# Input projections of an encoder layer as 2x2 block products with seven multiplications, in a phase of their own

## The chip, the cores and the metric

The kernel runs on one core of one Trainium2 chip. The metric is the device time of one execution in microseconds (us), the median of several runs. One further execution was profiled; rows and stage times come from it.

## The reference

One layer of a bidirectional encoder is applied with the same weights to two sequences, a prompt of 512 and a sample of 2048 tokens, all in float32, 1024 channels wide:

```python
h = rmsnorm(x, norm_pre)
z = h @ w_in                                  # 1024 -> 6656
pool_u, pool_g, q, k, v, attn_g, merge = split(z)   # 1024, 1024, 1024, 256, 256, 1024, 2048
pb = group_linear(windowed_mean(pool_u) - pool_u) * pool_scale * silu(pool_g)   # windows 2, 4, 8, 16
ab = windowed_attention(rope(q), rope(k), v, sink) * silu(attn_g)   # 16 heads, 4 kv heads, 64 wide, |i-j| <= 128
m = sigmoid(merge[:1024]) * (pb @ w_pool_proj) + sigmoid(merge[1024:]) * (ab @ w_attn_proj)
y = x + rmsnorm(m @ w_out, norm_post)
```

## The kernel before

Every float32 operand of a product is split into two parts, `hi` (rounded to the fp32r type of TensorE) and `lo` (the rest). `mm3` makes three products of each: hi x hi, hi x lo and lo x hi, lines 115 to 117. The split is `hi_lo`: a copy on ScalarE (L75) and a subtraction on VectorE (L76).

The tokens are worked in five blocks of 512, the prompt and four of the sample. A block is finished, from normalisation to output, before the next one begins. The normalised input `h` of a block lies in SBUF as 8 pairs of `hh`/`hl` tiles, 128 channels each. `unit` makes 128 output channels for the whole block: 8 pieces of 128 input channels, three products each, 24 products with a 128x128 weight tile as stationary operand and 512 tokens as moving one, summed in one PSUM bank, and then a `post` function. Weights are loaded from DRAM for each block again, 256 KB at a time (L82), and split again.

At the start `fold` multiplies the per-group maps of the pooling branch into the weights of `pool_u` and writes the product `wpool` to DRAM, 32 steps of six products of 256 columns.

A block runs in this order. `kv_phase` makes keys and values with tokens on the partitions, and transposes the keys. `q_units` makes and rotates the queries. Then attention runs: `grid` lays the steps of 16 groups (4 key heads x 4 query blocks of 128) into slots, and `mix` spreads other units evenly between them (queries of the next key head, `ag`, `ga`, `gp`, some `u`), 256 steps in all. A group computes scores (L334, L335), the masked maximum (L338), the exponentials (L340), scales them by the reciprocal sum (L353, L359 and L357), transposes them (L368), splits them into `pt`, and multiplies them by the values (L379, L380; results are added up in L387 to L390). The raw gates `ga` and `gp` go to DRAM and come back (L314, L433). After attention the block runs `ap_unit` (attention projection), the rest of `u_unit` with `pg_unit` (pooling branch), `pp_unit` (pooling projection) and `out_phase` (output projection, second norm, residual), 16 + 8 units and 64 steps. The statistics and the split of the next block's `h` are made meanwhile.

TensorE runs in the order in which the program is written; the last loop of `encoder` asks for the weights of the next `AHEAD = 2` items. The other engines' orders are set by a scheduler at compile time, from the same program. All transfers are issued by SyncE (SP), in one order.

## Time and profile before

| | us |
|---|---|
| median of 3 runs (2499.0 to 2502.37) | 2499.87 |
| span of the profiled execution | 2497.5 |
| TensorE busy | 2475.3 (99%) |
| VectorE busy | 1689.9 (68%) |
| ScalarE busy | 1381.8 (55%) |
| DMA, mean over the span | 129 GB/s, 322.60 MB |

The profiled execution's span lies 2.4 us below the median of the runs. Products overlap in the pipeline, so their durations add up to more than the busy time; distances between starts tell what one of them takes from the stream. L numbers are lines of the kernel before.

### The profile page before, as it was taken

What the parts mean: (1) busy time and instruction counts of PE and PEld (TensorE: products, weight loads), DVE (VectorE), ACT (ScalarE), POOL (GpSimd) and SP (SyncE); (2) the same over time, 40 slices, a digit from 0 to 9 for tenths busy, and PEclk for the clock granted to TensorE, in tenths of its full rate; (3) what the DMA queues carried; (4) which work ended last, traced back from release to release, by engine and by line L of the source; (5) the groups of instructions that cost most, each with busy time, mean ns of one, the idle gap of its engine ahead of it and who ended that gap; (6) DMA issues with size and microseconds to landing.
All of it is one profiled execution on the core that took longest, in us unless ns stands there. A gap on an engine that the chain in (4) does not pass through costs nothing.

```text
span 2497.5 us, 33882 instructions
## 1 busy us (share of the span) xinstructions
PE 2475.3 (99%) x11591; PEld 2039.2 (82%) x11591; DVE 1689.9 (68%) x3315; ACT 1381.8 (55%) x2831; POOL 117.7 (5%) x298
## 2 busy tenths in 40 slices
PE   8999999999999999999999999999999999999999
PEld 6888888878888888888888888888888878888887
DVE  5777756568777465777774657777746568776464
ACT  4777633437776333477763434776634357765342
POOL 0000100000000000000000000000000000000000
PEclk9999999999999999999999999999999999999999
DMA  7332473553224535522245445222454442334443
GB/s 231 98 93 91 140 232 108 169 167 94 85 95 130 173 101 162 179 89 89 85 127 177 127 150 164 89 85 89 133 167 141 142 153 81 91 89 155 131 160 106
DMA packets 179245, 322.60 MB, mean 129 GB/s; under 512 B 22144, under 2 KB 33664, under 8 KB 179072
## 3 DMA queue, kind: packets, MB, share of 16 engines
q1 hardware_dynamic: 179072, 320.43, 40.9%
q8 instruction: 91, 1.49, 0.2%
q14 instruction: 82, 0.67, 0.1%
HBM read 274.22 MB, written 46.14 MB: 128 GB/s over the span
## 4 chain that ended last, share of the span: by engine, by line
PE 95%; DMA 2%; DVE 1%; ACT 1%; issue 0%; SPq 0%; POOL 0%; DVEq 0%; POOLq 0%; ACTq 0%
PE ps_g L116 24%; PE ps_g L117 24%; PE ps_g L115 24%; PE ps_t L368 4%; PE ps_s L117 2%; PE ps_s L116 2%; PE ps_o L380 2%; PE ps_s L335 2%; PE ps_s L115 2%; PE ps_s L334 2%; PE ps_o L379 2%; PE ps_t L115 1%; PE ps_t L116 1%; PE ps_t L117 1%; DMA x<-in_x_sample 1%
## 5 line engine op out<-in xcount | busy, mean ns | idle before, releaser
L75 ACT CAST wh<-wr 128x512 fp32r<-128x512 f32 x776 | 478.6, 619 | 670.7 <-PE ps_g L116 326.7
L115 PE MATMUL ps_g<-hh,wh 128*128 128x512 f32 (+1 forms) x1920 | 770.0, 401 | 0.0
L117 PE MATMUL ps_g<-hh,wl 128*128 128x512 f32 (+1 forms) x1920 | 750.8, 391 | 0.3 <-DVE wl L76 0.3
L116 PE MATMUL ps_g<-hl,wh 128*128 128x512 f32 (+1 forms) x1920 | 749.8, 390 | 0.0
L76 DVE TENSOR_TENSOR wl<-wr,wh 128x512 fp32r<-128x512 f32 x776 | 531.0, 688 | 319.9 <-ACT wh L75 316.9
L117 PEld LDWEIGHTS ps_g<-hh,wl 128*128 128x128 f32 x1920 | 360.8, 188 | 82.3 <-DVE wl L76 1.0
L116 PEld LDWEIGHTS ps_g<-hl,wh 128*128 128x128 f32 x1920 | 361.7, 188 | 59.0
L115 PEld LDWEIGHTS ps_g<-hh,wh 128*128 128x128 f32 x1920 | 361.2, 188 | 57.7
L116 PE MATMUL ps_g<-A,wh 128*128 128x512 f32 x640 | 254.3, 397 | 0.0
L115 PE MATMUL ps_g<-A,wh 128*128 128x512 f32 x640 | 252.7, 395 | 0.0
L117 PE MATMUL ps_g<-A,wl 128*128 128x512 f32 x640 | 251.6, 393 | 0.0
L340 ACT ACTIVATE P<-ps_s,nm 128x384 f32<-128x384 f32 (+1 forms) x320 | 179.1, 560 | 123.8 <-DVE nm L338 121.6
L338 DVE CUSTOM_DVE_ANT_0 ps_s<-ps_s,mask,nsink 128x384 f32<-128x384 f32 (+1 forms) x320 | 190.0, 595 | 84.3 <-PE ps_s L335 81.9
L76 DVE TENSOR_TENSOR pt<-ps_t,pt 128x512 fp32r<-128x512 f32 x224 | 153.7, 687 | 32.5 <-ACT pt L75 29.3
L115 PEld LDWEIGHTS ps_g<-A,wh 128*128 128x128 f32 x640 | 120.2, 188 | 30.1
L117 PEld LDWEIGHTS ps_g<-A,wl 128*128 128x128 f32 x640 | 120.2, 188 | 29.0
L116 PEld LDWEIGHTS ps_g<-A,wh 128*128 128x128 f32 x640 | 120.2, 188 | 27.9
L368 PEld LDWEIGHTS ps_t<-ident,P 128*128 128x128 f32 x896 | 111.7, 141 | 29.5
L368 PE MATMUL ps_t<-ident,P 128*128 128x128 f32 x896 | 134.1, 272 | 0.0
L75 ACT CAST pt<-ps_t 128x512 fp32r<-128x512 f32 x168 | 97.1, 579 | 29.0 <-PE ps_t L368 28.9
L335 PE MATMUL ps_s<-ktl,q 128*128 128x384 f32 (+1 forms) x320 | 104.1, 325 | 0.0
L334 PE MATMUL ps_s<-kth,q 128*128 128x384 f32 (+1 forms) x320 | 103.7, 324 | 0.0
(240 smaller groups left out, 3278.1 us busy)
## 6 DMA issues: line engine op xcount, KB each, us to landing
wr<-in_w_q SPq DMA_DIRECT2D x80, 256.0 KB, 2.9
wr<-in_w_ag SPq DMA_DIRECT2D x80, 256.0 KB, 2.9
wr<-in_w_ga SPq DMA_DIRECT2D x80, 256.0 KB, 2.8
wr<-in_w_gp SPq DMA_DIRECT2D x80, 256.0 KB, 2.8
wr<-wpool SPq DMA_DIRECT2D x80, 256.0 KB, 2.7
wr<-in_w_ap SPq DMA_DIRECT2D x80, 256.0 KB, 3.2
wr<-in_w_pg SPq DMA_DIRECT2D x80, 256.0 KB, 2.7
wr<-in_w_pp SPq DMA_DIRECT2D x80, 256.0 KB, 2.9
```

What stands on the lines that cost most here:

```text
L75: (e.copy if e is A else e.tensor_copy)(hi, src)
L76: pick(key, 1).tensor_sub(lo, src, hi.bitcast(F32))
L115: T.matmul(o, lhsT=xs[0], rhs=ys[0], start=start, stop=False)
L116: T.matmul(o, lhsT=xs[0], rhs=ys[1], start=False, stop=False)
L117: T.matmul(o, lhsT=xs[1], rhs=ys[0], start=False, stop=stop)
L334: T.matmul(s, lhsT=q, rhs=kth[:, kv, kc], start=True, stop=False)
L335: T.matmul(s, lhsT=q, rhs=ktl[:, kv, kc], start=False, stop=True)
L338: V.tensor_tensor_reduce(s, s, mask[:, kb0 * 128:kb1 * 128], -1.0, nsink[:, H:H + 1], ALU.add, ALU.min, nm[:, h:h + 1])
L340: A.activation(P[:, 0:nk], s, AF.Exp, bias=nm[:, h:h + 1], scale=-1.0, accum_out=l[:, h:h + 1])
L368: T.transpose(tp[:, h * 128:(h + 1) * 128], pr[h][:, i * 128:(i + 1) * 128], cst["ident"])
L379: T.matmul(o, lhsT=v, rhs=pts[i][:, 0, :], start=i == 0, stop=False)
L380: T.matmul(o, lhsT=v, rhs=pts[i][:, 1, :], start=False, stop=i == kb1 - kb0 - 1)
```

## The change

The input projections are taken out of the block loop into a first phase. Weights are taken in 26 pairs of 128-wide units; a pair and a token block make a 2x2 by 2x2 block product: A is the pair's weights (two units by two halves of the 1024 input channels), B the block's `h` (two halves of the channels by two halves of the tokens). It is computed in Winograd's form of Strassen's scheme: seven products (M1 to M7) instead of eight, with sums S1 to S4 of weight blocks and T1 to T4 of input blocks as operands, and five additions behind them that use the PSUM bank's own accumulation where two products add up. Each product has 4 pieces of 128 channels and three matmuls each.

There are three token blocks over both sequences together: 768, 896 and 896 tokens, so the moving operand has 384, 448 and 448 columns. The seven moving operands of a block (`form`), split into hi and lo, lie in a fixed SBUF area, the `arena`. `h` is computed once per block, written to DRAM (`prep_h`) and read back in pieces. In the first block the weight sums are computed, split, and their split form is written to DRAM (`swd`); in the two later blocks it is loaded. The first two and the last two pairs run together as duos; in the last duo the operands of the next block are formed one by one.

Behind a pair a `Post` function finishes the result for all the block's tokens, and stores it in DRAM: `Rope` for keys and queries (rotation, split, 16 stores of 32 partitions), `Values` (transposes, split), `Silu`, `Gate` (sigmoid), `Pool` (window means times the gate). All 32 fold steps come ahead of the first pair.

The second phase takes the five blocks of 512 tokens again. Per key head `fetch_kv` loads split queries, keys, values and the attention gate. Attention is mixed with the pooling projection of the next block and the attention projection of the last one, 128 steps in all; the fifth block has 64. Then the output projection of the last block follows. The pooling result, the attention result and the half-finished merge go through DRAM, and are split as they come back (`put_set`).

```diff
+NPAIR = 26
+BLOCKS = ((0, 768), (768, 1664), (1664, 2560))
+HALF = 448
+ORDER = ("M1", "M6", "M2", "M5", "M7", "M3", "M4")
+WOP = {"M1": "A11", "M2": "A12", "M3": "S4", "M4": "A22", "M5": "S1", "M6": "S2", "M7": "S3"}
+XOP = {"M1": "B11", "M2": "B21", "M3": "B22", "M4": "T4", "M5": "T1", "M6": "T2", "M7": "T3"}
+SOPS = ("S2", "S1", "S3", "S4")
+XS = ("B11", "T2", "B21", "T1", "T3", "B22", "T4")
+NX = 7 * 2 * 4 * HALF
+AHEAD_H, AHEAD = 4, 3
+NW, NZ, NH, NR, NS_, NPB, NPT = 8, 6, 8, 2, 6, 8, 3
...
+    PS = {"g": 2, "s": 3, "t": 2, "o": 1}
...
+    arena = const.tile([128, NX], F32R, tag="arena", name="arena")
...
+    def prep_h(s, k):
+        a_, b = BLOCKS[s]
+        xk = ztile()
+        nc.sync.dma_start(xk[:, 0:b - a_], a["xt"][k, :, a_:b])
+        V.scalar_tensor_tensor(xk[:, 0:b - a_], xk[:, 0:b - a_], cst["gpre"][:, k:k + 1], rbc[s][:, 0:b - a_], ALU.mult, ALU.mult)
+        nc.sync.dma_start(hd[s][k], xk[:, 0:b - a_])
...
+        def piece(k, half):
+            t = htile()[:, 0:w]
+            nc.sync.dma_start(t, hd[s][k][:, half * w:(half + 1) * w])
+            return t
+
+        def put(r, k, src):
+            hi_lo(X[r][0][:, k, 0:w], X[r][1][:, k, 0:w], src)
+
+        for k in range(4):
+            if r == "B11":
+                put(r, k, piece(k, 0))
+            elif r == "B21":
+                put(r, k, piece(k + 4, 0))
+            elif r == "B22":
+                put(r, k, piece(k + 4, 1))
+            elif r == "T2":
+                b11, b12, b22 = piece(k, 0), piece(k, 1), piece(k + 4, 1)
+                V.tensor_sub(b12, b12, b11)
+                if k % 2 == 0:
+                    t2s["z"] = ztile()
+                t2 = t2s[k] = t2s["z"][:, k % 2 * 512:k % 2 * 512 + w]
+                V.tensor_sub(t2, b22, b12)
+                put("T2", k, t2)
...
+        def raw(self):
+            if self.R is not None:
+                return
+            self.R = self.p1.tile([128, 2048], F32, tag="R", bufs=NR, name="R")
+            for c0, c1, src in self.srcs:
+                if self.s > 0:
+                    c1 = min(c1, 1536)
+                nc.sync.dma_start(self.R[:, c0:c1], src[:, 0:c1 - c0])
+
+        def sums(self, n):
+            if n not in self.S:
+                a11, a12, a22, a21 = (self.R[:, i * 512:(i + 1) * 512] for i in range(4))
+                if n == "S1":
+                    op, x, y = V.tensor_add, a21, a22
+                elif n == "S3":
+                    op, x, y = V.tensor_sub, a21, a11
+                elif n == "S2":
+                    op, x, y = V.tensor_add, self.sums("S3"), a22
+                else:
+                    op, x, y = V.tensor_sub, a12, self.sums("S2")
+                t = self.p1.tile([128, 512], F32, tag="S", bufs=NS_, name="S")
+                op(t, x, y)
+                self.S[n] = t
+            return self.S[n]
+
+        def op(self, n):
+            self.raw()
+            if n[0] == "S" and self.s > 0:
+                w = wtile()
+                move(w, swd[self.n][SOPS.index(n)])
+                return w
+            src = self.sums(n) if n[0] == "S" else self.R[:, ("A11", "A12", "A22").index(n) * 512:][:, 0:512]
+            w = wtile()
+            hi_lo(w[:, 0, :], w[:, 1, :], src)
+            if n[0] == "S":
+                move(swd[self.n][SOPS.index(n)], w)
+            return w
...
+        for r in ORDER:
+            def f(r=r):
+                bank = {"M1": "A", "M2": "A", "M6": "B", "M5": "B", "M3": "B", "M7": "C", "M4": "C"}[r]
+                first = r in ("M1", "M6", "M7")
+                if first:
+                    st[bank] = psum(tags[bank])[:, 0:w]
+                acc = st[bank]
+                wt = pair.items[r].w
+                xh, xl = X[XOP[r]]
+                for k in range(4):
+                    c = slice(k * 128, (k + 1) * 128)
+                    mm3(acc, (wt[:, 0, c], wt[:, 1, c]), (xh[:, k, 0:w], xl[:, k, 0:w]), first and k == 0, k == 3, not first)
+                if r == "M1":
+                    st["s"] = htile()[:, 0:w]
+                    A.copy(st["s"], acc)
+                elif r == "M6":
+                    st["U2"] = htile()[:, 0:w]
+                    V.tensor_add(st["U2"], acc, st["s"])
+                elif r == "M2":
+                    post.start()
+                    for dst, c in post.dst(0, 0):
+                        post.first(dst, acc[:, c])
+                    post.done(0, 0)
+                elif r == "M5":
+                    st["U4"] = htile()[:, 0:w]
+                    V.tensor_add(st["U4"], acc, st["s"])
+                elif r == "M7":
+                    add(1, 1, acc, st["U4"])
+                elif r == "M3":
+                    add(0, 1, acc, st["s"])
+                else:
+                    add(1, 0, acc, st["U2"])
+                    post.finish()
+                if after is not None:
+                    after(r)
+            steps.append((pair.items[r], f))
...
+        def finish(self):
+            W = self.W
+            x1, x2 = (z[:, 0:W] for z in self.z)
+            cs, sn = rope[0][:, 0, 0:W], rope[0][:, 1, 0:W]
+            t1, t2 = ztile()[:, 0:W], ztile()[:, 0:W]
+            V.tensor_mul(t1, x1, cs)
+            V.tensor_mul(t2, x2, sn)
+            V.tensor_sub(t1, t1, t2)
+            V.tensor_mul(x2, x2, cs)
+            V.tensor_mul(x1, x1, sn)
+            V.tensor_add(x2, x2, x1)
+            for c, y in enumerate((t1, x2)):
+                hi = ztile(F32R)[:, 0:W]
+                lo = y.bitcast(F32R)
+                hi_lo(hi, lo, y)
+                for e, z in enumerate((hi, lo)):
+                    rows = slice((2 * e + c) * 32, (2 * e + c + 1) * 32)
+                    for h in range(4):
+                        move(self.to[rows, h, self.a:self.b], z[32 * h:32 * h + 32, :])
...
+        def finish(self):
+            for z, f in zip(self.z, self.fs):
+                nc.sync.dma_start(self.to[f][:, self.a:self.b], z[:, 0:self.W])
...
+                specs += [g[x] for x in (("q", "ag", "u0", "gp", "u1", "ga") if kv < 3 else ("q", "u0", "ag", "u1", "gp", "ga"))]
+            pairs = [Pair(p1, s, n, sr) for n, sr, _ in specs]
+            duos = [[0, 1]] + [[i] for i in range(2, NPAIR - 2)] + [[NPAIR - 2, NPAIR - 1]]
+            extra = {3: vals.tr_steps()}
+            if nxt:
+                extra[12] = [(None, lambda s=s: stats(s + 1))]
+                extra[15] = [(None, lambda s=s: prep_r(s + 1))]
+                for k in range(NKT):
+                    extra[16 + k // 2] = extra.get(16 + k // 2, []) + [(None, lambda s=s, k=k: prep_h(s + 1, k))]
+            prog.append((None, lambda s=s: load_rope(p1, s, "rope_k")))
+            for duo in duos:
+                if duo[0] == 2:
+                    prog.append((None, lambda s=s: load_rope(p1, s, "rope_q")))
+
+                def after(r, last=nxt and duo[-1] == NPAIR - 1, s=s):
+                    if last:
+                        form(s + 1, XOP[r])
+                steps = [pair_steps(pairs[i], specs[i][2], j, after if j + 1 == len(duo) else None) for j, i in enumerate(duo)]
+                ahead = [i for i in range(duo[-1] + 1, min(duo[-1] + 2, NPAIR))]
+                for j in range(7):
+                    for x in steps:
+                        prog.append(x[j])
+                    if j == 0:
+                        prog.append((None, lambda ahead=ahead, pairs=pairs: [pairs[i].raw() for i in ahead if len(ahead) == 1]))
+                for i in duo:
+                    prog += extra.get(i, [])
...
+    SETS = [(region(o, 8, 512), region(o + 4096, 8, 512)) for o in (0, 8192)]
+    QT = [region(16384 + i * 2048, 4, 512) for i in range(2)]
+    KT = [[region(20480 + i * 1536 + e * 768, 768) for e in range(2)] for i in range(2)]
+    VT = [region(23552 + i * 768, 6, 128) for i in range(2)]
...
+        def put_set(n, k, src):
+            t = htile()
+            nc.sync.dma_start(t, src)
+            hi_lo(SETS[n][0][:, k, :], SETS[n][1][:, k, :], t)
...
+            move(q, qd[kv][:, :, g0:g0 + TB])
+            for r in range(2):
+                rows = slice(64 * r, 64 * r + 64)
+                move(kh[rows, 0:c], kd[0:64, kv, lo:hi])
+                move(kl[rows, 0:c], kd[64:128, kv, lo:hi])
+            move(v[:, 0:c // 128, :], vd[:, kv, lo // 128:hi // 128, :])
...
+        prog = [(None, lambda: fetch_kv(0, 0))]
+        prog += [(None, f) for f in pp_puts(0, 1)]
+        for n in range(5):
+            x, y = (n % 2, 1 - n % 2) if n < 4 else (1, 0)
+            if n == 0:
+                fill = spread(pp(0, 1), pp_puts(1, 0)) + spread(pp(1, 0), pp_puts(2, 1))
+            elif n < 4:
+                fill = spread(pp(n + 1, x), ap_puts(n - 1, y)) + ap(n - 1, y, x)
             else:
...
+                fill = ap(n - 1, y, x)
+            if n == 0:
+                prog += fill[:9]
+                fill = fill[9:]
+            prog += mix(fill, grid([attn_group(n, kv, b) for kv in range(NKV) for b in range(4)]))
+            if n > 0:
+                early = pp_puts(n + 2, y) if n < 3 else ap_puts(n, y)
+                prog += spread(out_phase(n - 1, x, False), early)
+        prog += ap(4, 0, 1)
+        prog += out_phase(4, 1, True)
+        return prog
+
     with tc.manual_schedule(engines={T.engine}):
...
+        with tc.tile_pool(name="p1", bufs=1) as p1:
+            run(phase1(p1), AHEAD_H)
+        with tc.tile_pool(name="p2", bufs=1) as p2:
+            run(phase2(p2), AHEAD)
...
```

## Rows read from the trace of the kernel before

**Rows 1.** The page: busy time, TensorE's slices, shares of the chain that ended last.
```profile
PE 2475.3 (99%) x11591; PEld 2039.2 (82%) x11591; DVE 1689.9 (68%) x3315; ACT 1381.8 (55%) x2831; POOL 117.7 (5%) x298
...
PE   8999999999999999999999999999999999999999
...
PE 95%; DMA 2%; DVE 1%; ACT 1%; issue 0%; SPq 0%; POOL 0%; DVEq 0%; POOLq 0%; ACTq 0%
PE ps_g L116 24%; PE ps_g L117 24%; PE ps_g L115 24%; PE ps_t L368 4%; PE ps_s L117 2%; PE ps_s L116 2%; PE ps_o L380 2%; PE ps_s L335 2%; PE ps_s L115 2%; PE ps_s L334 2%; PE ps_o L379 2%; PE ps_t L115 1%; PE ps_t L116 1%; PE ps_t L117 1%; DMA x<-in_x_sample 1%
```

**Rows 2.** Timeline of TensorE at four places: start us, duration us, what.
```profile
901.51 0.28 PE L117 MATMUL ps_s<-hh,wl 128*128 128x260 f32 x1
...
905.83 0.28 PE L117 MATMUL ps_s<-hh,wl 128*128 128x260 f32 x1
...
999.88 0.39 PE L115 MATMUL ps_s<-wh,q 128*128 128x512 f32 x1
...
1005.48 0.39 PE L115 MATMUL ps_g<-wh,q 128*128 128x512 f32 x1
...
1201.63 0.34 PE L334 MATMUL ps_s<-kth,q 128*128 128x384 f32 x1
...
1201.99 0.39 PE L115 MATMUL ps_g<-hh,wh 128*128 128x512 f32 x1
...
1203.37 0.60 PE L368 MATMUL ps_t<-ident,P 128*128 128x128 f32 x4
...
1204.05 0.40 PE L116 MATMUL ps_g<-hl,wh 128*128 128x512 f32 x1
```

**Rows 3.** Timeline of VectorE in two attention stretches.
```profile
106.94 0.69 DVE L76 TENSOR_TENSOR wl<-wr,wh 128x512 fp32r<-128x512 f32 x1
107.55 0.69 DVE L76 TENSOR_TENSOR pt<-ps_t,pt 128x512 fp32r<-128x512 f32 x1
108.15 0.62 DVE L338 CUSTOM_DVE_ANT_0 ps_s<-ps_s,mask,nsink 128x384 f32<-128x384 f32 x1
...
108.68 0.69 DVE L76 TENSOR_TENSOR wl<-wr,wh 128x512 fp32r<-128x512 f32 x1
...
1198.29 1.22 DVE L393 TENSOR_TENSOR x<-x 128x1024 f32<-128x1024 f32 x1
1199.42 0.68 DVE L76 TENSOR_TENSOR wl<-wr,wh 128x512 fp32r<-128x512 f32 x1
```

**Rows 4.** The page's groups: one of the three lines of input units.
```profile
L115 PE MATMUL ps_g<-hh,wh 128*128 128x512 f32 (+1 forms) x1920 | 770.0, 401 | 0.0
```

**Rows 5.** Stretches: length, busy us by engine, granted clock, DMA share, GB/s.
```profile
0.00:40.00 40.00, 27.64 (x125) 23.15 (x126) 21.18 (x34) 18.75 (x31) 1.40 (x6) 0.87 0.85 268
10.00:20.00 10.00, 7.34 (x36) 6.05 (x35) 5.73 (x9) 6.41 (x12) 1.21 (x2) 0.82 0.78 269
20.00:30.00 10.00, 7.83 (x47) 7.11 (x47) 5.83 (x9) 2.96 (x5) 0.00 (x0) 0.84 0.96 285
25.00:35.00 10.00, 5.84 (x29) 4.57 (x30) 6.12 (x10) 2.87 (x6) 0.00 (x0) 0.92 0.85 254
100.00:150.00 50.00, 50.00 (x250) 41.73 (x249) 41.84 (x95) 38.48 (x89) 2.54 (x7) 1.00 0.28 90
```

**Rows 6.** DMA issues: KB each, median us from issue to landing.
```profile
wr<-in_w_q SPq DMA_DIRECT2D x80, 256.0 KB, 2.9
```

**Rows 7.** VectorE's groups by shape: busy us, mean ns of one, idle before.
```profile
L338 DVE CUSTOM_DVE_ANT_0 ps_s<-ps_s,mask,nsink 128x384 f32<-128x384 f32 x256 | 158.7, 621 | 55.1 <-PE ps_s L335 53.0
L76 DVE TENSOR_TENSOR pt<-ps_t,pt 128x512 fp32r<-128x512 f32 x224 | 153.7, 687 | 32.5 <-ACT pt L75 29.3
L359 DVE TENSOR_SCALAR P<-P,l 128x384 f32<-128x384 f32 x192 | 69.2, 416 | 1.3
L389 DVE TENSOR_TENSOR x<-x,ps_o 64x256 f32<-64x256 f32 x80 | 33.0, 412 | 59.2 <-ACT x L388 52.3 <-PE ps_s L335 6.7
L393 DVE TENSOR_TENSOR x<-x 128x1024 f32<-128x1024 f32 x20 | 24.4, 1221 | 0.1
```

**Rows 8.** SP's own waits: us in total, times, longest.
```profile
SPq L314 <- ACT f L312: 162.2, 69, 6.1
```

1101 lines of the change are left out of this document (545 added, 556 removed).

## The prediction

> **What bounds the kernel now.** I read the page's busy line first, then the slices, then the chain. TensorE is busy for 2475.3 of 2497.5 us, VectorE for 68% of the span and ScalarE for 55% [rows 1]; the slices put TensorE at 9 everywhere but in the first, and the chain that ended last is 95% TensorE, three quarters of it products into ps_g [rows 1]. So a TensorE column taken away is time won, as long as nothing else becomes the limit. What the busy share can't tell is what one product costs, since products overlap. For that I take distances between starts: 24 products of 512 columns start within 5.60 us, 233.3 ns each; 36 of 260 columns within 4.32 us, 120 ns; two of 384 within 0.36 us, 180 ns [rows 2]. A straight line through the first and the second gives 0.45 ns a column and 3 ns on top, so 448 columns cost 204.5 ns and 384 cost 175.8 (the row says 180). There is almost no fixed price per product, so narrower products lose next to nothing.
>
> The same reading is needed for VectorE. One 512-wide split lasts 0.69 us, but the next instruction starts 0.61 us after it; the masked maximum lasts 0.62 and is followed after 0.53; a 1024-wide one lasts 1.22 and is followed after 1.13 [rows 3]. I call this distance its slot: 0.075 us and 1.035 ns a column. Where an instruction needs the one before it, about 0.09 us come on top.
>
> **What the change removes.** Before, 48 input units of 24 products over five blocks, 1920 in each of three lines [rows 4], of which 192 have 504 columns and 384 have 260: 1344.5 us. Keys and values add 20 token tiles x 8 x 3 = 480 products of 512, 112.0 us. Together 1456.5 us. After, 26 pairs x 7 products x 4 pieces x 3 = 2184 in each token block: 383.7 us at 384 columns and twice 446.6 us at 448, 1277.0 us. That is **-179.5 us**. Key transposes go (20 groups), value transposes come (11 groups); a group of four takes 0.45 us (1203.37 to 1204.05 less one product [rows 2]), **-4 us**. The products of fold, attention, pool, attention and output projection stay.
>
> What is left to ask is where TensorE now waits. I go by stage.
>
> **The start.** Before, TensorE was busy for 27.6 of the first 40 us, at 268 GB/s and a mean clock of 0.87 [rows 5]; 12.4 us were lost. Now h is written to DRAM and read back to form the seven moving operands, and all 32 fold steps come ahead of the first product. Up to the end of the first two pairs the queue carries x 3.1 MB, fold weights 6.3, fold stores 4.2, xt 3.1, h out 3.1, 44 pieces back 8.7, raw weights 2.1, split sums out 4.2, tables 1.3: 36.1 MB. The rows bound the rate: 285 GB/s at a share of 0.96 and 269 at 0.78 make 297 to 345 when full [rows 5]; 36 MB need 105 to 122 us. TensorE's work in that time is 192 x 0.12 + 168 x 0.176 = 52.5 us. Some of the stores need not have landed, so I take 57 us lost, **+45** on before. Bounds: 27 MB at 345 GB/s, +15; all of it at the 254 GB/s of the poorest 10 us [rows 5], +77.
>
> **First token block (383.7 us of products).** VectorE, in slots: a pair has 7 splits and 4 weight sums of 0.61 and 5 accumulator adds of 0.47, 9.1 us; a Rope pair 7.2 more, Silu 1.7, Values 2, Pool 5.6 on average. Over 26 pairs 326 us, and 34 for preparing the next block: 361 us, 94%. DMA: a pair reads 1.05 MB and writes 2.10 of split sums, outputs are 22 MB, the next block's preparation 21: 125 MB, 362 to 421 us. Two resources about as full as TensorE and an order that ties them together: 8 us for the middle of the DMA bounds and 20 for the coupling, **+28**, bounds +5 and +60.
>
> **Second and third block (893 us).** Sums are now loaded: 3 splits instead of 7, VectorE at about 60%, DMA 123 MB and 102 MB in 447 us each, 276 and 228 GB/s, below the 297. What is late here is the turn of a block: the last two Pool pairs leave some 15 us on VectorE, while the new operands are split, and accumulator adds stand behind Rope's eight wide instructions. **+20**, bounds +6 and +50.
>
> **Turn to the second phase.** The operand sets lie over the old moving operands and can be filled only when the last products have read them; a load takes 2.9 us to land [rows 6], then eight splits, then queries and keys. **+15**, bounds +8 and +25.
>
> **Attention mixed with projections.** TensorE per block: scores 21.5, values 20.9, transposes 224 x 0.45 / 5 = 20.2, and 128 fill steps x 3 x 0.2333 = 89.6: 152 us (107 in the last block, which has half the fill). VectorE slots per block from [rows 3, 7]: maxima 32.9, scaling 16.3, splits of pt 27.3, adds from ps_o 14.1, reciprocals and ot 6.4, together 97 (over five blocks 256 maxima and 192 scalings 384 wide, 64 and 48 more 256 wide at 0.41 and 0.26, 224 splits, 80 pairs of adds at 0.44); fill 72 x 0.61 = 43.9. That is 141 of 152, and 122 of 107 in the last block. Before, VectorE was busy for 41.8 of 50 us in such a stretch and TensorE lost nothing [rows 5]. So the last block is bound by VectorE: +15, and 5 for its ends; the four others at about 90% lose some 6 each. **+43**, bounds +15 and +110 (rival two). The output stages stay bound by TensorE (44.8 us against some 25).
>
> **A rule against the change.** The loads and stores that I read, such as [rows 6], move 128 partitions; Rope now stores in pieces of 32 partitions and keys are fetched in 64. The rows have no price for that; my sum takes the full rate. The Trainium skill, "SBUF — State Buffer", section "Door 1: The DMA port swizzle", says that 32 or 64 partitions reach only half of the ports and about half of the bandwidth; no run here shows it yet. By it Rope's stores would count twice.
>
> **Sum.** -179.5 - 4 + 45 + 28 + 20 + 15 + 43 = -32.5 us on the profiled span of 2497.5, 2465. The median of the runs shown is 2.4 us above that span, so I predict **2467 us**, 1.3% faster. With each term by half of its bounds this case spans 2430 to 2500. A measurement of this kernel tells about 0.2% from no change.
>
> **Rivals.**
>
> One: stores bar the issuing queue (slower). All transfers go out on SP's queue in one order. After a Rope pair 16 stores wait for eight VectorE instructions of about 1.0 us (9 us with the waits between), then take 0.33 to 0.5 us each to issue, 15 us in all, while weights are asked for four operands ahead, 4 x 12 x 0.2045 = 9.8 us, and need 3 us to land: 8 us late, at 15 Rope pairs, +120, **2587 us**. It decides from 33 / 15 = 2.2 us a pair. For it: 69 gate stores held SP for 162 us before, up to 6.1 at a time [rows 8]. Against it: TensorE lost nothing by that, and the order on the queue is not that of the program. Chance 0.17.
>
> Two: VectorE is the limit in attention. By durations instead of slots [rows 7] the same work is 115 + 72 x 0.69 = 164 us against 152 in a block with full fill and 142 against 107 in the last; with the ends, where only products run, +100 to +125 instead of +43: **2537 us**. For it: dependent instructions do pay the whole duration. Against it: the slots. Chance 0.11.
>
> Three: nearly everything is hidden. All terms at their low bounds: +49, **2365 us**. For it: the kernel before hides VectorE at 84% without loss [rows 5]. Against it: 36 MB at the start can't be hidden. Chance 0.17.
>
> Four: Rope's stores run at half rate. They are 7.9 MB in the first block, where DMA has no room: at some 315 GB/s another 25 us, **2492 us**, within a hair of no change. (This is the rule of the page named above.) No row speaks for or against it. Chance 0.08, counted as no change.
>
> **How the numbers follow.** The sum has 0.47. Range 2400 to 2590: it leaves out the lower half of rival three and the upper half of rival one, 0.17 together. Faster by over 0.2%: 0.47 + 0.17 = 0.64; within it 0.08; slower 0.17 + 0.11 = 0.28.
>
> **What would show it.** Starts of products 204 and 176 ns apart in the first phase (if 384 and 448 columns cost more, the main term is wrong). TensorE's busy time near 2290 us. The first product on a moving operand after about 60 us, and the first pairs over at 105 to 120. In the first block DMA share above 0.85 and TensorE idle for some 30 us; in the second and third nearly none but at the turns; if TensorE waits there for loaded sums, behind stores on SP, it is rival one. In the second phase VectorE above 90% and TensorE waiting for it mostly in the last attention block; if in all of them, rival two. I would be wrong for a reason outside this list if ScalarE (some 128 of 152 us in attention) set the pace, or if the granted clock fell in stretches in which TensorE waits often, as it did from 10 to 30 us, to means of 0.82 and 0.84 between its two levels of 1.2 and 2.4 GHz [rows 5].

## The result: 5% slower, and the profile after

The kernel after takes 2623.9 us (median of 4 runs, 2620.35 to 2628.05) against 2499.43 of the kernel before beside it (4 runs): 1.0501 times as long, 95% interval 1.0486 to 1.0516. The forecast was 2467, and its range ended at 2590. The profiled execution of the kernel after has a span of 2619.8 us.

The page of the kernel after, to be laid beside [rows 1]: busy times, TensorE's slices and granted clock in tenths, DMA, the chain that ended last. In the rows PE is TensorE, DVE VectorE, ACT ScalarE, POOL GpSimd and SPq the queue of SyncE; L numbers are now lines of the kernel after, or of the run that a row is from.

```profile
PE 2367.9 (90%) x11668; PEld 2096.9 (80%) x11668; DVE 1772.0 (68%) x3382; ACT 1133.9 (43%) x2445; POOL 97.2 (4%) x294
...
PE   2579988878899999889999989999999999988999
...
PEclk8789998988899999999999999999999999999999
...
DMA packets 246832, 593.49 MB, mean 227 GB/s; under 512 B 28800, under 2 KB 65408, under 8 KB 244352
...
PE 58%; DVE 10%; DMA 6%; ACT 4%; issue 2%; SPq 1%; POOL 0%; DVEq 0%; POOLq 0%; ACTq 0%
```

TensorE was 95% of the chain and is 58%. It is busy for 107 us less, but stands idle for 252 us (2619.8 - 2367.9) where it stood for 22. A slice is 65.5 us: the holes lie in the first eleven (720 us) and in the 17th and 18th, those later on are few.

Stretches of the kernel after, cut where TensorE's timeline shows the first product on a moving operand (104.9), the end of the first two pairs, of each token block, and of the first phase. Columns as in [rows 5].

```profile
0.00:104.90 104.90, 30.13 (x199) 28.74 (x199) 64.02 (x107) 39.84 (x73) 1.73 (x6) 0.72 0.91 297
104.90:134.50 29.60, 29.60 (x171) 29.60 (x169) 21.46 (x37) 10.97 (x20) 0.00 (x0) 1.00 0.78 290
134.50:585.40 450.90, 386.48 (x2036) 378.18 (x2036) 326.15 (x549) 164.38 (x295) 15.06 (x50) 0.92 0.72 250
585.40:1084.90 499.50, 461.08 (x2208) 421.24 (x2207) 268.01 (x400) 138.74 (x237) 1.71 (x2) 0.96 0.74 252
1084.90:1558.70 473.80, 454.19 (x2200) 415.85 (x2199) 247.06 (x376) 123.81 (x205) 5.53 (x16) 0.99 0.67 226
1558.70:2619.80 1061.10, 1006.42 (x4864) 823.27 (x4862) 845.34 (x1916) 656.17 (x1617) 73.19 (x220) 0.98 0.61 196
```

The forecast in the same cuts: the first pairs over at 109.5 (52.5 of products and 57 lost), the first block 382 (354.4 of products behind the first pairs, and 28), the two others 913 (893 + 20), the rest 1060.5; in sum 2465. The rest holds the 5 us of value transposes, which run in the first phase. Measured: 134.5, 450.9, 973.3, 1061.1. So the first phase is 25 + 69 + 60 us late, less these 5: nearly the whole error.

Who TensorE waited for, over the whole span (waiting engine and line, the engine that ended the wait; us in total, times, longest):

```profile
PE ps_g L110 <- DVE h L162: 59.8, 5, 57.1
PE ps_s L110 <- DVE h L323: 37.2, 11, 5.8
PE ps_s L110 <- DVE h L331: 23.2, 3, 13.2
PE ps_s L110 <- DMA w<-sw_S: 19.9, 4, 10.4
...
PE ps_s L110 <- DVE z L303: 17.7, 8, 7.0
```

L162 is the fold's evacuation at the start. L323 (U2), L331 (U4) and L303 are the accumulator adds. Waits that a transfer ended are 20 us only.

One such wait in the first block, on VectorE (behind a Rope pair) and on TensorE:

```profile
366.93 0.96 DVE L418 TENSOR_TENSOR z<-z 128x768 f32<-128x768 f32 x1
367.80 0.96 DVE L419 TENSOR_TENSOR z<-z,rope 128x768 f32<-128x768 f32 x1
...
371.00 0.69 DVE L277 TENSOR_TENSOR S<-R,S 128x512 f32<-128x512 f32 x1
371.61 0.96 DVE L80 TENSOR_TENSOR z<-z 128x768 fp32r<-128x768 f32 x1
372.47 0.70 DVE L80 TENSOR_TENSOR w<-S,w 128x512 fp32r<-128x512 f32 x1
373.07 0.56 DVE L323 TENSOR_TENSOR h<-ps_s,h 128x384 f32<-128x384 f32 x1
```

```profile
367.54 0.34 PE L112 MATMUL ps_g<-arena,w 128*128 128x384 f32 x1
373.69 0.69 PE L110 MATMUL ps_s<-arena,w 128*128 128x384 f32 x1 [5.81 <-DVE h L323]
374.18 0.52 PE L111 MATMUL ps_s<-arena,w 128*128 128x384 f32 x1
374.50 0.52 PE L112 MATMUL ps_s<-arena,w 128*128 128x384 f32 x1
...
378.28 0.33 PE L112 MATMUL ps_s<-arena,w 128*128 128x384 f32 x1
378.46 0.34 PE L110 MATMUL ps_s<-arena,w 128*128 128x384 f32 x1
```

VectorE runs without a pause: rotation, weight sums and splits of the next pair, and only then the add that TensorE needs. TensorE idles for 5.8 us, and then its products start 0.32 us apart instead of 0.18 until 378.0. The stretches show why:

```profile
371.00:373.00 2.00, 0.00 (x0) 0.00 (x0) 2.00 (x4) 1.78 (x5) 0.00 (x0) 0.59 0.72 171
373.00:375.00 2.00, 1.31 (x4) 1.31 (x5) 2.00 (x5) 0.39 (x1) 0.00 (x0) 0.50 0.88 209
375.00:377.00 2.00, 2.00 (x8) 2.00 (x7) 1.97 (x4) 0.75 (x2) 0.00 (x0) 0.50 0.88 209
```

The granted clock has gone to the lower of its levels (0.50 is 1.2 GHz) while the engine idled. Over the first block TensorE is idle for 64 us (450.9 - 386.5) and its busy time is 32 us above the 354.4 of its products: about a third of the block's loss. Of these 32 us, 23 are some 160 products that start about 0.32 us apart, and 1.4 are transposes of values.

VectorE's pile-up begins with raw weights that landed late. ScalarE waited 5.5 us for them. Their load was issued behind two gate stores, for whose data SP had stood 8.4 us (SP's wait from 340 to 351 us, the issue, ScalarE's wait):

```profile
SPq L381 <- ACT z L377: 8.4, 2, 6.5
...
350.64 0.45 SPq L263 DMA_DIRECT2D R<-in_w_h  x1
...
359.18 0.62 ACT L79 CAST w<-R 128x512 fp32r<-128x512 f32 x1 [5.51 <-DMA R<-in_w_h]
```

### The profile page after: what moved, and what is told of

It reads as the page before. It is cut to its first block, busy times and chain, and to the rows that moved or that the text cites. A ratio compares the mean times of both kernels' runs of the same rounds, so it can differ in the third digit from the quotient of the medians.

```text
span 2619.8 us, 34621 instructions
## 1 busy us (share of the span) xinstructions
PE 2367.9 (90%) x11668; PEld 2096.9 (80%) x11668; DVE 1772.0 (68%) x3382; ACT 1133.9 (43%) x2445; POOL 97.2 (4%) x294
## 4 chain that ended last, share of the span: by engine, by line
PE 58%; DVE 10%; DMA 6%; ACT 4%; issue 2%; SPq 1%; POOL 0%; DVEq 0%; POOLq 0%; ACTq 0%
PE ps_s L110 9%; PE ps_s L111 8%; PE ps_s L112 8%; PE ps_g L111 7%; PE ps_g L112 7%; PE ps_g L110 7%; PE ps_t L810 2%; DMA h<-h 2%; DVE ps_s L786 1%; PE ps_o L823 1%; ACT P L788 1%; PE ps_s L782 1%; PE ps_o L822 1%; PE ps_s L783 1%; DVE pt L80 1%
## 5 line engine op out<-in xcount | busy, mean ns | idle before, releaser
L110 PE MATMUL ps_s<-arena,w 128*128 128x448 f32 (+1 forms) x1512 | 555.6, 367 | 98.3 <-DVE h L323 37.2
L112 PE MATMUL ps_s<-arena,w 128*128 128x448 f32 (+1 forms) x1512 | 550.8, 364 | 0.5 <-DVE w L80 0.5
L111 PE MATMUL ps_s<-arena,w 128*128 128x448 f32 (+1 forms) x1512 | 551.0, 364 | 0.0
L110 PE MATMUL ps_g<-arena,w 128*128 128x512 f32 (+2 forms) x1264 | 493.6, 391 | 13.4 <-ACT arena L79 7.5
L112 PE MATMUL ps_g<-arena,w 128*128 128x512 f32 (+2 forms) x1264 | 481.6, 381 | 3.3 <-DVE w L80 3.2
L111 PE MATMUL ps_g<-arena,w 128*128 128x512 f32 (+2 forms) x1264 | 481.8, 381 | 0.8 <-DVE arena L80 0.8
L110 PEld LDWEIGHTS ps_s<-arena,w 128*128 128x128 f32 x1512 | 293.3, 194 | 124.7 <-DVE h L323 37.5
L303 DVE TENSOR_TENSOR z<-ps_s,h 128x448 f32<-128x448 f32 (+3 forms) x230 | 133.6, 585 | 262.3 <-PE ps_s L112 261.3
L112 PEld LDWEIGHTS ps_s<-arena,w 128*128 128x128 f32 x1512 | 292.9, 194 | 17.7 <-DVE w L80 0.9
L111 PEld LDWEIGHTS ps_s<-arena,w 128*128 128x128 f32 x1512 | 293.6, 194 | 16.4
L79 ACT CAST w<-R 128x512 fp32r<-128x512 f32 x234 | 141.3, 619 | 307.0 <-PE ps_s L112 243.1
L112 PEld LDWEIGHTS ps_g<-arena,w 128*128 128x128 f32 x1264 | 242.2, 192 | 39.9 <-DVE w L80 4.6
L110 PEld LDWEIGHTS ps_g<-arena,w 128*128 128x128 f32 x1264 | 242.6, 192 | 36.4 <-ACT arena L79 8.4
L111 PEld LDWEIGHTS ps_g<-arena,w 128*128 128x128 f32 x1264 | 242.8, 192 | 22.8 <-DVE arena L80 1.5
L80 DVE TENSOR_TENSOR w<-wr,w 128x512 fp32r<-128x512 f32 x232 | 158.6, 687 | 103.1 <-ACT w L79 102.1
L79 ACT CAST w<-wr 128x512 fp32r<-128x512 f32 x232 | 143.6, 619 | 158.5 <-PE ps_t L112 51.2
L80 DVE TENSOR_TENSOR w<-R,w 128x512 fp32r<-128x512 f32 x234 | 158.6, 688 | 53.7 <-ACT w L79 50.6
L79 ACT CAST arena<-h 128x512 fp32r<-128x512 f32 (+2 forms) x192 | 111.5, 593 | 140.3 <-DMA h<-h 43.8
```

The lines of the kernel that those rows point to most:

```text
L79: A.copy(hi, src)
L80: V.tensor_sub(lo, src, hi.bitcast(F32))
L110: T.matmul(o, lhsT=xs[0], rhs=ys[0], start=start, stop=False, skip_group_check=more)
L111: T.matmul(o, lhsT=xs[0], rhs=ys[1], start=False, stop=False, skip_group_check=more)
L112: T.matmul(o, lhsT=xs[1], rhs=ys[0], start=False, stop=stop, skip_group_check=more)
L303: V.tensor_add(dst, acc[:, c], t[:, c])
```

## The experiments

Each run is given by its median, its ratio to the kernel before (in the runs beside it), and by stage times from its trace. For comparison, the kernel after: **2623.9, 1.0501; first block 450.9; second and third 973.3.**

### The pair's end behind the next pair's adds

`finish` is made a generator that yields between its parts; the next pair runs a part after each of its adds.

```diff
+                    drain(1)      # after the U2 add, and after the U4 add
...
+                    drain()       # after the M7 add
...
-                    post.finish()
+                    pending.append(post.finish())
```

> Edit: what a pair does at its end (Rope, Pool, the gates' stores) no longer stands on VectorE ahead of the next pair's accumulator adds, but is cut into pieces that follow the next pair's U2 add, its U4 add and its M7 add. The work and the bytes are the same. Order theory (the 59.8 + 37.2 us that TensorE waits for an h tile on VectorE are an order of one queue, and each wait is followed by some us at the low clock): the first block falls from 450.9 us by 35 to 55, the second and third together by 10 to 25, the whole from a span of 2619.8 to about 2555 (2535 to 2575). Saturation theory (VectorE at some 94% in the first block and DMA as full, so order doesn't matter): the first block stays within 10 us of 451, the whole above 2605.

Measured: 2578.9, 1.0313 (1.0297 to 1.0328). First block 428.2, the others 956.1. Half-way between the theories in the first block: waits for U2 adds there go (26.9 to 1.8 us), but waits of up to 9.1 us for the adds into z come up, and the wait for the U4 add at the first turn grows from 13.2 to 17.0. The whole lies just above the order theory's 2575.

### The adds first in VectorE's order, nothing else

```diff
-                    V.tensor_add(st["U2"], acc, st["s"])
+                    with tc.high_priority(300):
+                        V.tensor_add(st["U2"], acc, st["s"])
```

(The same for U4 and for the adds into z.)

> Edit: the accumulator adds of phase one (U2, U4 and the adds of M7, M3, M4) are given a higher priority in the compiler's scheduler; the program, its work and its bytes are otherwise unchanged. In VectorE's order the U2 add of a pair behind Rope then stands after four of its wide instructions instead of after all eight, at some of the pairs. If the order alone makes the waits: the 26.9 us for U2 adds in the first block fall below 12, and the first block by 12 to 25 us, the whole to about 2605. If the adds are late because the instructions in front of them are themselves late (splits that wait for tiles or loads): first block within 8 us, the whole within 8 us of 2624.

Measured: 2612.2, 1.0463 (1.0447 to 1.0479); first block 442.2. TensorE's waits in that run from 136 to 530 us:

```profile
PE ps_s L110 <- DVE z L304: 12.8, 5, 7.0
PE ps_g L110 <- ACT w L79: 10.2, 4, 6.9
PE ps_g L112 <- DVE w L80: 9.8, 3, 7.7
PE ps_s L112 <- DVE w L80: 6.5, 8, 3.4
```

The U2 add is down to 0.5 us, and the splits of weights, pushed back, appear. The block is 8.7 us shorter, between the two theories. This order is worth 9 us and that of the run before 23, so the order of VectorE's queue is a part of the loss and not the whole; that VectorE has too much to do at such places, whatever comes first, is the reading of both.

### Less work for VectorE: split sums loaded in the first block too

```diff
-                if self.s > 0:
+                if self.s > 0 or self.n > 1:
                     c1 = min(c1, 1536)
...
-            if n[0] == "S" and self.s > 0:
+            if n[0] == "S" and (self.s > 0 or self.n > 1):
                 w = wtile()
-                move(w, swd[self.n][SOPS.index(n)])
+                move(w, swd[self.n % 2][SOPS.index(n)])
```

> Edit: 24 of the 26 pairs of the first block load their four split weight sums too, as the later blocks do, from those that the first two pairs wrote (the true sums of these pairs are left out, so the values are other ones, in all three blocks). It takes 8 VectorE instructions of 0.61 us from each of 24 pairs, 117 us in all, and turns the stores of 2.1 MB a pair into as many bytes of loads. Saturation of VectorE: the first block falls from 450.9 to 385 to 400 us, nearly its products alone, the whole to about 2560. Saturation of DMA: no change in the first block (within 10 us). Order theory: waits behind Rope and Pool get shorter, since fewer splits stand in front too, but do not go: some 2 to 3 us at 13 pairs and the clock after them, so the first block falls to 405 to 425 and the whole to some 2580 to 2590.

Measured: 2575.8, 1.0295 (1.028 to 1.031); first block 407.6, the others 973.0. DMA as a limit by bytes is out here: nearly as many bytes (108 MB against 113) run at 266 GB/s instead of 250. But the 43.3 us are not VectorE's work alone: the stores of sums, which wait on SP's queue for VectorE's splits (119 us of SP's waits from 134 to 545 us in the kernel after), are gone too. With the pairs' ends moved as well:

> Edit: the two edits that helped, in one: the pair's end cut into pieces behind the next pair's adds, and split sums loaded by 24 of 26 pairs of the first block from those of the first two (the true sums are left out). Alone they took 22.7 and 43.3 us from the first block's 450.9. If order and amount are two sides of the same overload of VectorE, they don't add: the first block comes to 400 to 410 us, and what is left is the turn. If they are separate losses they add: 385 us or less.

Measured: 2551.6 (one run), first block 395.9. The edits took 22.7 and 43.3 us alone and take 55.0 together: by this one execution most of it adds, and the first block lies between the two expectations.

### Less to store, VectorE's work unchanged

The stores of sums are left out for 24 of 26 pairs.

```diff
-                move(w, swd[self.n][SOPS.index(n)])
+                move(w, swd[self.n % 2][SOPS.index(n)])
...
-            if n[0] == "S":
+            if n[0] == "S" and self.n < 2:
                 move(swd[self.n][SOPS.index(n)], w)
```

> Edit: 24 of 26 pairs of the first block make and split their weight sums as before but don't store them, and later blocks load those of the first two pairs (the true sums are left out there, so the values are other ones): 2.1 MB a pair, 50 MB, less traffic in the first block, VectorE's work unchanged. If DMA (share 0.64 to 0.83 there) sets part of the first block's time, it falls from 450.9 by 25 us or more, the whole below 2600. If only VectorE's work does, as the loaded sums and the pieces of the pairs' ends suggest, the first block stays within 10 us of 451 but for a shorter first turn; the whole 2610 to 2625.

Measured: 2579.7, 1.0312 (1.0296 to 1.0327); first block 415.1. My second theory, VectorE's work alone, falls too. The block's stretch, and the landing of raw weights from 135 to 545 us:

```profile
133.50:548.60 415.10, 371.67 (x2037) 366.11 (x2036) 329.09 (x554) 170.15 (x299) 13.91 (x50) 0.95 0.49 159
```

```profile
R<-in_w_h SPq DMA_DIRECT2D x14, 1024.0 KB, 5.2
```

VectorE is busy for 329 us as before (326), at a DMA share of 0.49 instead of 0.72. Raw weights land in 5.2 us where the kernel after has 6.8, and ScalarE's waits for those of `w_h` (136 to 545 us) fall from 17.1 to 6.7 us. That the sums and splits then start earlier and no longer fall upon the end of the pair before is an inference. To tell bytes from the w tiles that a store holds, a copy within DRAM takes each store's place:

```diff
...
+            elif n[0] == "S":
+                nc.sync.dma_start(swd[self.n][SOPS.index(n)], a["w_h"][self.n % 18][:, 0:1024].rearrange("p (e c) -> p e c", e=2))
```

> Edit: as in the run without stores of sums (first block 415.1 us, whole 2580), but in the place of each store a copy of as many bytes from one place of DRAM to another is issued, which holds no tile (true sums left out, values are other ones). If the 36 us that the missing stores gave are bytes (the other loads land later while the queue is full): the first block goes back to 440 to 455 and the whole to about 2615. If they are the w tiles that a store holds until it has landed (eight w tiles, four of seven operands stored, 3.6 us to landing and the wait for SP's queue before): the first block stays at 415 to 425 and the whole below 2592.

Measured: 2603.8, 1.0426 (1.041 to 1.0441); first block 438.3. Of the 35.8 us, 23 come back with the bytes; some 13 stay away. They can be the tiles, or SP's waits for split sums, which a copy doesn't have either: this run doesn't separate them. A copy takes 8.6 us to land where a store took 3.6, so it is no exact stand-in. The scheduler orders VectorE anew in each of these runs, which by the run on priority can be worth 9 us, so the shares are rough.

### Half the bytes, nothing left out

Sums are stored and loaded as plain numbers, and split again in later blocks.

```diff
-    swd = [[scratch(f"sw{p}_{n}", [128, 2, 512]) for n in SOPS] for p in range(NPAIR)]
+    swd = [[scratch(f"sw{p}_{n}", [128, 512]) for n in SOPS] for p in range(NPAIR)]
...
-                w = wtile()
-                move(w, swd[self.n][SOPS.index(n)])
+                src = self.p1.tile([128, 512], F32, tag="S", bufs=NS_, name="S")
+                nc.sync.dma_start(src, swd[self.n][SOPS.index(n)])
+                w = wtile()
+                hi_lo(w[:, 0, :], w[:, 1, :], src)
...
-                move(swd[self.n][SOPS.index(n)], w)
+                nc.sync.dma_start(swd[self.n][SOPS.index(n)], src)
```

> Edit, complete: the sums are stored and loaded as plain 32-bit numbers instead of as split pairs, half the bytes (1.05 MB a pair instead of 2.1), held by an S tile instead of a w tile, and split again in the later blocks (there 4 more splits a pair on VectorE and ScalarE, 2.4 us a pair beside 17.2 us of products). First block by the run without these stores: 20 to 36 us less. Second and third: if VectorE had room there (steady stretches lose nothing with some 35% idle), unchanged or up to 10 us less at the turns; if not, 10 us or more worse. The whole 2585 to 2605.

Measured: 2564.0, 1.0277 (1.0257 to 1.0297): 60 us below the kernel after, more than expected. First block 411.1, the others 956.2. A steady stretch of its second block, then the same of the kernel after:

```profile
700.00:1000.00 300.00, 299.70 (x1472) 275.23 (x1471) 210.46 (x310) 123.77 (x211) 1.71 (x2) 1.00 0.61 201
```

```profile
700.00:1000.00 300.00, 298.45 (x1465) 274.41 (x1464) 157.63 (x232) 82.35 (x136) 1.71 (x2) 1.00 0.76 259
```

VectorE goes from 53 to 70% busy there and TensorE still loses nothing, with Rope and Pool ends in it.

### The sums on GpSimd

```diff
-                    op, x, y = V.tensor_add, a21, a22
+                    op, x, y = G.tensor_add, a21, a22
...
```

> Edit: the four weight sums of each pair of the first block run on GpSimd, which is busy for 4% of the span, instead of on VectorE. It takes 104 x 0.61 = 63 us off VectorE in the first block, at unchanged bytes and order. If VectorE's amount of work sets the first block: about half of what the loaded sums gave (43.3 us), so 15 to 25 us less, the whole near 2605. If GpSimd is so slow that the sums come late (more than some 3 us each), or takes VectorE's time by sharing its way to the buffer: no change or slower, with waits of the splits for S tiles in the trace. No row of before or after shows this operation on GpSimd at this size.

Measured: 2672.9, 1.07 (1.0684 to 1.0716); first block 499.8, 49 more. Groups of that run:

```profile
L277 POOL TENSOR_TENSOR S<-R 128x512 f32<-128x512 f32 x52 | 79.9, 1538 | 280.8 <-DMA R<-in_w_h 116.3 <-DMA wpool<-h 77.4 <-DMA R<-in_w_pg 69.5
```

```profile
L80 DVE TENSOR_TENSOR w<-S,w 128x512 fp32r<-128x512 f32 x104 | 91.8, 900 | 23.8 <-ACT w L79 22.9
...
L303 DVE TENSOR_TENSOR z<-ps_s,h 128x384 f32<-128x384 f32 x66 | 36.6, 554 | 45.6 <-PE ps_s L112 44.6 <-ACT z L180 0.6 <-DMA q<-z 0.2
```

A sum takes 1.54 to 1.67 us on GpSimd instead of 0.69. And VectorE's splits of sums last 900 ns instead of 688 on average, those of raw weights 769 instead of 688 (907 in the first block), while the adds with one input in PSUM keep theirs (554, before 556). The Trainium skill, "SBUF — State Buffer", section "Who interferes with whom", says that a VectorE operation with two SBUF inputs contends with a GpSimd one that reads SBUF, over a port pair that one of them holds at a time. This trace agrees: two-input forms got longer, and those with an input in PSUM didn't. Two small copies with one input got longer too (L484, 128x16: 542 ns in the first block, before 172), which that statement doesn't cover. How much of the 49 us is late sums and how much longer splits wasn't taken apart, so the run doesn't say what less work for VectorE is worth.

### The start

The second half of the fold ahead of the forming of operands:

```diff
-            for r in XS:
-                form(0, r)
...
-        prog += fs[16:]
+        prog += fs[16:28]
+        for i, r in enumerate(XS):
+            prog.append((None, lambda r=r: form(0, r)))
+            prog += fs[28 + i:29 + i]
```

> Edit: at the start the second half of the fold runs before the operands of the first block are formed, with the last four steps between them, instead of after all 44 pieces. Order theory (the 57.1 us wait of the fold's evacuation is for h tiles that the pieces in front of it hold, and nothing is on TensorE meanwhile): the first two pairs are over at 100 to 110 us instead of 134.3, the whole 25 to 35 us less, about 2590. Rival, the start is bound by bytes (298 GB/s at a share of 0.91 between 0 and 100 us): the fold is done early, the wait comes instead before the first pair, the first pairs are over at 127 to 134, the whole 0 to 8 us less.

Measured: 2624.3, 1.0486 (1.0468 to 1.0503). The first product on a moving operand comes at 88.4 instead of 104.9, and the first pairs end at 136.3. The start is as long as before, so the order theory of the 57 us wait is out. Next, the fold out of the start:

```diff
-        prog += fs[0:16]
         prog.append((None, second))
-        prog += fs[16:]
...
+            if s == 0:
+                extra[1], extra[2] = fs[0:16], fs[16:32]
```

> Edit: the fold of the pool weights (6.3 MB in, 4.2 MB out, 192 products of 256 columns) does not run at the start but after the first two pairs and after the third, ahead of the first Pool pair. Theory that the start is bound by bytes (38.6 MB in the first 130 us of the kernel after, 297 GB/s): the first product on a moving operand comes at 65 to 75 us instead of 104.9 and the first two pairs end near 100 instead of 134.5; the fold's bytes then go under products of the first block, whose DMA share is 0.64 to 0.83, and the first block starts later products 10 to 25 us earlier: the whole 10 to 25 us less, 2600 to 2615. Rival (the start is bound by the chain from x over the row sums, h out and h back, whatever the bytes): first product not before 90 us, the whole within 8 us or slower, since VectorE takes 24 us of the fold's work in the middle.

Measured: 2614.6, 1.0467 (1.0451 to 1.0482). The first product on a moving operand comes at 35.8, the first pairs end at 99.4:

```profile
0.00:99.40 99.40, 35.46 (x175) 33.80 (x176) 56.36 (x98) 36.37 (x68) 1.73 (x6) 0.85 0.84 294
```

The kernel after moved 295 GB/s up to 134.5. 10.5 MB less at that rate are 35.6 us, and the first pairs end 35.1 us sooner: the start goes by bytes. (The edit also takes 192 products and some 24 us of VectorE's work out of the start; that the saving equals the bytes is what speaks for them.) But the first block ends at 581.7 instead of 585.4; the gain is given back in it.

### The turns between blocks

The next block's operands formed one product later:

```diff
-                        form(s + 1, XOP[r])
+                        i = ORDER.index(r)
+                        for x in ORDER[max(i - 1, 0):i + (i == 6)] if i else ():
+                            form(s + 1, XOP[x])
```

> Edit: at the turn of a block each moving operand of the next block is formed one product later, so that the accumulator add after M5 stands ahead of the twelve loads and splits of T2 on VectorE. Order theory: the waits for the U4 add at the two turns (13.2 and 9.7 us) go, and with them some of the low clock behind: 15 to 30 us less over the second and third block, the whole 2590 to 2605. Rival, the turn is bound by its loads (44 pieces through eight h tiles): the wait moves to the first products of the next block, change within 8 us either way.

Measured: 2619.5, 1.0474 (1.0459 to 1.049): no change. Pieces in the idle S tiles instead of h tiles:

```diff
-            t = htile()[:, 0:w]
+            t = (cst["p1"].tile([128, 512], F32, tag="S", ...) if s > 0 else htile())[:, 0:w]
```

> Edit: the pieces of h that form the operands of the second and third block go into the S tiles, which are free at that time, instead of the eight h tiles, six of which hold s, U2 and U4 of the two pairs that run at the turn. Tile theory (the turn is slow because only two h tiles are left and T2 needs three pieces at a time, so that loads are not asked for in time and VectorE waits in its order for each): the waits for the U4 add (13.2 and 9.7 us) fall below 4 us each, those for split sums behind them (10.4 and 4.0) get shorter, the three blocks together lose 25 to 40 us, the whole from 2624 to 2585 to 2600. Rival (the turn is full of bytes and VectorE work, as the later forming of the operands that changed nothing suggests): within 8 us of 2624.

Measured: 2618.0, 1.0473 (1.0455 to 1.049): within the rival's 8 us; a wait of 14 us stays, now for ScalarE's half of the split of a weight. The tile theory falls. How VectorE stands there in the kernel after:

```profile
562.16 0.63 DVE L235 TENSOR_TENSOR z<-h 128x448 f32<-128x448 f32 x1 [1.82 <-DMA h<-h]
...
566.55 0.62 DVE L235 TENSOR_TENSOR z<-h 128x448 f32<-128x448 f32 x1 [1.69 <-DMA h<-h]
...
570.99 0.62 DVE L235 TENSOR_TENSOR z<-h 128x448 f32<-128x448 f32 x1 [1.64 <-DMA h<-h]
...
573.98 1.02 DVE L331 TENSOR_TENSOR h<-ps_s,h 128x384 f32<-128x384 f32 x2
```

A part of T2 every 4.4 us, each waiting for its pieces, and then the U4 add for which TensorE waited 13.2 us. So the loads themselves are taken away, three of four, with the instructions kept:

```diff
+            if s > 0 and (k // 4, half) in kept:
+                return kept[k // 4, half]
...
```

> Edit: at the two turns an operand's pieces are loaded once and used for all four of its parts (the other three parts are left out, so the values are other ones): 11 loads of 229 KB instead of 44 at each turn, 7.6 MB less, with the same VectorE and ScalarE instructions in the same order. If what holds the turn is the pieces' arrival (272 to 285 GB/s from 550 to 600 us, VectorE and ScalarE waiting in their order for each piece), the waits for the U4 add (13.2 and 9.7 us) and for split sums (10.4 and 4.0) go below 3 us each, the three blocks together lose 25 to 45 us, the whole 2580 to 2600. If it is the turn's VectorE work (some 26 us of differences and splits beside the adds), change within 10 us.

Measured: 2604.8, 1.0407 (1.0389 to 1.0424). The waits for the U4 add go from 13.2 and 9.7 us to 4.2 and none, those for loaded sums from 19.9 us in all to 9.0; waits of 10.4 us for the copy of M1 (L320 in the kernel after, 1.4 there) come up. From the end of the first pairs to that of the phase it takes 1400.0 us instead of 1424.2; another 10 us were lost at the start, where the forms take one more tile. Taking away 33 of the 44 pieces is thus worth 24 us at both turns, 13 of them in the first block, in which the first turn's wait lies.

### Complete versions

Each is made of diffs above. Plain sums and the pairs' ends moved:

> Edit, complete: the plain sums and the pair's end in pieces behind the next pair's adds (alone -45 us). If stores and order are two ways to relieve the same waits: 2560 to 2575. If they add: 2535 to 2550. In no case below the kernel before (2499), since the start (57 us), the turns and the second phase (58 us over its products) are not touched.

Measured: 2558.3, 1.0243 (1.0227 to 1.0258). Relieving DMA and moving the ends meet in the same waits. With the fold later as well:

> Edit, complete: plain sums, pairs' ends in pieces, and the fold after the first pairs instead of at the start. If the start's lost time is bytes and the first block had no room to take the fold's (14 us won at the start, 10 given back there, when only the fold was moved), then with half the sums' bytes gone the gain stays: 12 to 20 us below the 2558 without it, 2538 to 2546. If the fold's VectorE work (24 us) was what the first block gave back: within 6 us of 2558.

Measured: 2554.6, 1.0214 (1.0199 to 1.023): the best version, still slower than the kernel before. The first block ends 4.1 us earlier (539.9 instead of 544.0). Without the moved ends:

> Edit, complete: plain sums and the fold after the first pairs, the pairs' ends where they were. By bytes: 12 to 20 us below the 2564 of plain sums alone, 2544 to 2552. By VectorE's work, which is then the same and in the same order as with plain sums but for the fold: 2558 to 2570.

Measured: 2563.5, 1.0249 (1.0232 to 1.0267), nothing over plain sums. With DMA relieved the fold's gain is still given back, which fits the second reading (no VectorE time for it in the first block) and not the first. An earlier combination with split sums:

> Edit: a complete version with three edits that leave nothing out: the pair's end in pieces behind the next pair's adds (alone -45 us in the median), the fold after the first pairs (-9), the turn's pieces in S tiles (-6). If they add: 2564. If they meet in the same waits: 2570 to 2580. Slower than the kernel before by at least 2.5% either way: the products saved are worth 179.5 us, and the losses that these edits don't touch (the rest of the first block, the turns, the second phase) are over 180.

Measured: 2582.0, 1.0319 (1.0301 to 1.0337), slower than both expectations and no better than the moved ends alone.

## Why the prediction was wrong, step by step

**The products: right.** From the timeline of the kernel after, 9 products of 384 columns in 1.59 us (0.177) and 6 of 448 in 1.23 us (0.205):

```profile
229.89 0.34 PE L110 MATMUL ps_s<-arena,w 128*128 128x384 f32 x1
...
231.48 0.34 PE L110 MATMUL ps_s<-arena,w 128*128 128x384 f32 x1
```

```profile
800.16 0.37 PE L110 MATMUL ps_s<-arena,w 128*128 128x448 f32 x1
...
801.39 0.36 PE L110 MATMUL ps_s<-arena,w 128*128 128x448 f32 x1
```

So the saving of 179.5 us holds wherever the products run at the full clock.

**The start (57 us lost): right mechanism, 25 us too small.** Bytes set it, as the fold's removal shows. I took 36.1 MB to be over by 109.5 us, which is 330 GB/s; the chip moved 39.7 MB up to the end of the first pairs at 134.5, at 295 GB/s. The 297 GB/s at a share of 0.91 make 326 when full, inside what I had scaled from [rows 5]; what the sum had wrong is a full share (it was 0.91, then 0.78) and 3.6 MB too few. The sign named for it failed too: the first product on a moving operand came at 104.9, not at about 60.

**The first block (+28): the step that failed most, 69 us.** Its text named two resources about as full as TensorE and an order that ties them, and priced the tie at 20 us, from no row. The loss was 96.5, of which 13.2 are the first turn's wait (at 574 us). The amount of work was right: VectorE is busy for 326 us beside 354.4 us of products, 92% where the forecast had 94%. But stretched over 451 us neither resource is full (DMA share 0.72, where a sign above 0.85 was named), and still TensorE waits, because the work falls in bursts: raw weights land late, and then the sums, splits and the end of the pair before stand in one queue ahead of the adds. Half the stored bytes took 40 us back, no stores 36, moving the pairs' ends 23, the adds' priority 9, and loaded sums, which take away VectorE's work and the stores together, 43. An average can't price that. The upper bound, +60, was too low as well. Through what the stores delay VectorE stays open: by bytes, by the tiles that they hold, or by their place on SP's queue.

**Second and third block (+20): wrong in size and in part in place, 60 us.** From 700 to 1000 us, with the other query pairs in it, TensorE is idle for 1.6 us in all. But behind the first query pair of each of these blocks the U2 add does stand behind them, as the text had it:

```profile
664.34 0.74 PE L110 MATMUL ps_s<-arena,w 128*128 128x448 f32 x1 [5.12 <-DVE h L323]
```

The waits are 58 us: 10.4 behind the first turn and 9.7 at the second, twice 5.1 for this add, twice 4.8 where transposes of values wait for their splits, 4.0 and 4.8 for loaded sums 73 and 60 us ahead of a block's end, and smaller ones. Another 22 us are longer busy time, 3.6 of them transposes of values. The turn was named; what I missed is that its 44 pieces arrive while DMA already moves 276 to 284 GB/s (550 to 600 us), and VectorE and ScalarE wait for each in their order. Fewer pieces gave 24 us at both turns together; the rest was not taken apart.

**The clock: named as outside the list, and it came.** Behind each wait of some 5 us the products run on at the lower level. In the first block it is 23 of the 32 us of longer busy time, and TensorE's total is 2367.9 instead of the 2290 forecast.

**Phase two (+15 and +43): right in sum, not place by place.** 1061.1 against 1055.5 (1060.5 without the value transposes), and TensorE is idle for 54.7 us where 58 were forecast. But the turn costs 7 us and not 15, and three waits of 4.4, 4.3 and 5.0 us, for the evacuation of the output stage (L694) where the next block's attention begins, were not in the list; that the sum agrees is partly luck. Attention in the third and the last block:

```profile
2000.00:2050.00 50.00, 49.40 (x254) 41.41 (x253) 46.99 (x112) 36.21 (x92) 2.62 (x12) 1.00 0.61 186
...
2350.00:2400.00 50.00, 42.66 (x210) 33.97 (x210) 42.75 (x110) 34.65 (x94) 2.90 (x12) 0.93 0.40 124
```

VectorE at 94% hides under TensorE there; in the last block's attention (2342 to 2480 us) TensorE is idle for 18 us, where 15 and 5 for its ends were forecast. Slots, not durations, were the measure, and rival two is out.

**The rivals.** One (stores bar the queue) gave a time near the measured one, but not where it was priced: waits for loaded sums are 20 us, not 120, and the two that come ahead of a block's end were for loads issued behind a store of Pool, not of Rope. So its mechanism is there, at stores of Gate and Pool. In the first block it is the late issue at 350.64 shown above. In the second, SP stands 12.5 us at a store of Pool with the loads of sums behind it, no transfer runs from some 999 to 1007 us, and TensorE waits:

```profile
SPq L512 <- DVE z L511: 12.5, 1, 12.5
...
1012.13 0.47 PE L110 MATMUL ps_s<-arena,w 128*128 128x448 f32 x1 [3.95 <-DMA w<-sw_S]
```

No run lets loads pass the stores that wait, so what this is worth in the first block is not known. Three is out. Four: where only Rope's stores are under way (272 to 277 us, in the run without sum stores as in the kernel after) they move 197 GB/s at a share of 0.83, 237 scaled to a full one; stores of sums reach 362 at 0.98 in the kernel after (377 to 379). The Trainium skill, "SBUF — State Buffer", section "Door 1: The DMA port swizzle", has about half the bandwidth for them; here the ratio is 0.54 as measured and 0.64 for full shares, so the trace agrees in kind. (The stores also differ in size, 96 against 512 KB, which no run separates.) TensorE is busy without a break in that stretch.

## What to carry to other kernels

Fewer products pay only where the engines that feed them have room in every few microseconds, not on average: look at what a queue holds in the 10 us ahead of each dependent add, and at when its inputs land. What a saving of TensorE time adds in bytes and VectorE work should be priced at the start, the first block and the turns, where most of it comes at once. Look also at which store a load stands behind on the issuing queue. In the first block the waits cost a third as much again behind them (23 us behind 64), because the clock falls.

## What the runs showed of the hardware

With the sums on GpSimd (1.54 us for 128x512), VectorE's splits of sums, with two SBUF inputs, took 900 instead of 688 ns on average, its adds with an input in PSUM the same as before. Stores of 32 partitions (96 KB each) ran at 237 GB/s scaled to a full share, where 128-partition stores (512 KB) ran at some 370. After 5.8 us of idling TensorE's products of 384 columns started 0.32 us apart for 4.3 us, at a granted clock of 0.50.
